# A fifth of the attention's probabilities transposed on TensorE, in a two-layer trunk on one core

## The chip, the cores and the metric

The kernel runs on one core of one Trainium2 chip. The metric is the device time of one execution in microseconds (us); less is better. Times of the kernel before are given as the median of three runs and as one profiled execution.

## The reference

The trunk has two layers on 2048 tokens of width 1024. Layer 0 mixes tokens by sliding-window attention, layer 1 by multi-head latent attention; behind each stands a mixture of experts. The change lies in layer 1's attention, for 16 heads with 64 + 32 columns of query and key and 64 of value:

```python
def block(args):
    qi, blk = args
    sc = jnp.einsum('bqhd,bkhd->bhqk', qi, k).astype(jnp.float32) * scale
    qpos = blk * Q_BLOCK + jnp.arange(Q_BLOCK)
    sc = jnp.where(kpos[None, :] <= qpos[:, None], sc, -jnp.inf)
    p = jax.nn.softmax(sc, axis=-1)
    return jnp.einsum('bhqk,bkhd->bqhd', p.astype(v.dtype), v)
```

`Q_BLOCK` is 128, so a head has 16 query blocks; block i looks at i + 1 key blocks.

## The kernel before

Float32 values are carried as two float16 tiles, a high and a low half, and a product is made of three matmuls. `attend` (L1333) does the attention of layer 1. A **unit** is one head h and one query block i. The list `units` takes, for each head, the query blocks in the order 15, 0, 14, 1, and so on; the last head takes them from 0 to 15. A unit's scores are computed in **chunks** of up to 512 keys (up to four **blocks** of 128), so two units in a row mostly have five chunks. There are 256 units, 640 chunks and 2176 blocks.

`scores` (L1381) does one chunk: three matmuls into a PSUM tile `sc` of a ring of seven (L1394 to L1396), a mask for the unit's last chunk (L1398), and the maximum of each row on DVE (L1399). Behind the last chunk DVE joins the maxima (L1404), and for each chunk ACT makes the exponential `bpr` (L1408). The probabilities must then stand with keys on the partitions, to be the stationary operand of the value matmuls. For this each chunk gets a place in a **pack** of up to 16 blocks: its high half is cast into `bpp` by DVE (L1422) or ACT (L1424), its low half is subtracted by POOL or DVE (L1425). The two shares in `SHARES` set how often DVE does the one or the other. A full pack goes out as one transposing transfer from `bpp` to `bpt`, issued on SP's queue by `turn` (L180). There are four buffers of `bpp` and five of `bpt`.

Chunks for which `direct` says so go another way. Before, these are the last three units of the last head. `turn_unit` (L1429) transposes their float32 blocks on PE against the identity (L1435) into another tile of the `sc` ring; ACT copies the high half out of PSUM (L1439) and DVE makes the low half (L1440).

`values` (L1442) multiplies a unit's transposed blocks with the values: for each block one matmul with the high half (L1454) and one with the low half (L1455), summed in the PSUM tile `po`. At a pair's end DVE reduces `po` to `ou` (L1461). `finish` normalises a pair of heads and transposes it with smaller transfers (`oT`).

The main loop goes over the units n. It calls the scores of unit n and the values of unit n - LAG, LAG being 4, chunk by chunk in turns, and behind them `turn_unit` of unit n - 1:

```python
for c in range(max(ns, nv)):
    if c < ns:
        scores(n, h, i, U[n], c)
    if c < nv:
        values(hv, iv, n - LAG, U[n - LAG], c)
if n - 1 in U and U[n - 1]["pr"]:
    turn_unit(U[n - 1])
```

The order of the instructions in each engine's queue is not just that of these calls: it is set while the program is built, by a scheduler that reckons with its own times of the engines. On the chip each queue runs in that order.

Of the kernel before, what the change touches and what calls it, by code (L numbers as in the profile page):

```python
# [12 lines left out]
F16 = mybir.dt.float16  # L13
# [8 lines left out]
P = 128  # L22
# [5 lines left out]
B_H, QR, KVR, NOPE, ROPE = 16, 384, 256, 64, 32  # L28
# [92 lines left out]
class Kernel:  # L121
# [1211 lines left out]
    def attend(self, q_d, kr_d, o_d, w_o):  # L1333
        nc, tc = self.nc, self.tc
        V, G, C = nc.vector, nc.gpsimd, nc.scalar
        LAG, PACK, SHARES = 4, 16, (1 / 3, 1 / 6)
        with ExitStack() as s:
            kp = s.enter_context(tc.tile_pool(name="tb", bufs=1, reuse_waits="tile"))
            wk = s.enter_context(tc.tile_pool(name="tk", bufs=2, reuse_waits="tile"))
# [3 lines left out]
            qb = [self.t(kp, [96, 2, S], F16, f"qb{n}") for n in range(2)]  # L1343
            for n in range(3):
                nc.sync.dma_start(kb[n][NOPE:], kr_d)
            U, heads, todo, owed = {}, {}, [], [0.0, -150.0]

            pack = {"n": 0}

            def room():  # L1350
                return self.t(ps, [P, 512], F32, "sc", bufs=7)

            def place(nb):
                if pack["n"] + nb > PACK:
                    send()
                if pack["n"] == 0:
                    pack["pp"] = self.t(wk, [P, PACK, 2, P], F16, "bpp", bufs=4)
                    pack["pt"] = self.t(wk, [P, PACK, 2, P], F16, "bpt", bufs=5)
                at = pack["n"]
                pack["n"] += nb  # L1360
                return pack["pp"][:, at:at + nb], pack["pt"][:, at:at + nb]

            def send():
                n, pp, pt = pack["n"], pack["pp"], pack["pt"]
                if n:
                    self.turn(pt[:, :n].rearrange("p k s q -> p (k s) q"), pp[:, :n].rearrange("p k s q -> p (k s q)"))
                pack["n"] = 0
# [6 lines left out]
                for u in range(2):  # L1374
                    nc.sync.dma_start(qb[e][64 + 16 * u:80 + 16 * u], q_d[g, 2][64 * u + 16 * n:64 * u + 16 * n + 16])

            def direct(h, i):

                return h == B_H - 1 and i >= 13

            def scores(n, h, i, u, c):  # L1381

                (Qh, Ql), (Kh, Kl) = ([b[h % len(b)][:, x] for x in range(2)] for b in (qb, kb))
                qs = slice(i * P, (i + 1) * P)
                nk = (i + 1) * P
                ncn = -(-nk // 512)
                if c == 0:
                    u["sm"], u["sc"], u["pt"], u["pr"] = self.t(wk, [P, 8], F32, "bsm2", bufs=4), [], [], []
                sm = u["sm"]
                w = min(512, nk - 512 * c)  # L1390
                ks = slice(512 * c, 512 * c + w)
                sc = room()
                last = c == ncn - 1
                nc.tensor.matmul(sc[:, :w], Qh[:, qs], Kh[:, ks], start=True, stop=False)  # L1394
                nc.tensor.matmul(sc[:, :w], Qh[:, qs], Kl[:, ks], start=False, stop=False)  # L1395
                nc.tensor.matmul(sc[:, :w], Ql[:, qs], Kh[:, ks], start=False, stop=not last)  # L1396
                if last:
                    nc.tensor.matmul(sc[:, w - P:w], self.ident_b, self.causal, start=False, stop=True)  # L1398
                V.tensor_reduce(sm[:, c:c + 1], sc[:, :w], axis=AX.X, op=ALU.max, negate=ncn == 1)  # L1399
                u["sc"].append((sc, w))  # L1400
                if not last:
                    return
                if ncn > 1:
                    V.tensor_reduce(sm[:, 4:5], sm[:, 0:ncn], axis=AX.X, op=ALU.max, negate=True)  # L1404
                nm = sm[:, 4:5] if ncn > 1 else sm[:, 0:1]
                for sc, w in u["sc"]:
                    pr = self.t(wk, [P, 512], F32, "bpr", bufs=7)
                    C.activation(pr[:, :w], sc[:, :w], AF.Exp, bias=nm)  # L1408
                    if direct(h, i):
                        u["pr"].append((pr, w))  # L1410
                        continue
                    pp, pt = place(w // P)
                    u["pt"].append(pt)
                    pb = pr[:, :w].rearrange("p (k q) -> p k q", q=P)

                    mine = [False, False]
                    for part, share in enumerate(SHARES):
                        owed[part] += share * w
                        if owed[part] > w / 2 and not (part and mine[0]):
                            mine[part], owed[part] = True, owed[part] - w  # L1420
                    if mine[0]:
                        V.tensor_copy(pp[:, :, 0], pb)  # L1422
                    else:
                        C.activation(pp[:, :, 0], pb, AF.Copy)  # L1424
                    (V if mine[1] else G).tensor_tensor(pp[:, :, 1], pb, pp[:, :, 0], op=ALU.subtract)  # L1425
                if n % 2 and (h == B_H - 1 or n == len(units) - 1):
                    send()

            def turn_unit(u):  # L1429

                pt = self.t(wk, [P, PACK, 2, P], F16, "bpt", bufs=5)
                for c, (pr, w) in enumerate(u["pr"]):
                    tp = room()
                    for k in range(0, w, P):
                        nc.tensor.transpose(tp[:, k:k + P], pr[:, k:k + P], self.ident)  # L1435
                    out = pt[:, 4 * c:4 * c + w // P]
                    u["pt"].append(out)
                    tp = tp[:, :w].rearrange("p (k q) -> p k q", q=P)
                    C.activation(out[:, :, 0], tp, AF.Copy)  # L1439
                    V.tensor_tensor(out[:, :, 1], tp, out[:, :, 0], op=ALU.subtract)  # L1440
# [63 lines left out]
            for n in range(len(units) + LAG):  # L1504
                ns = nv = 0
                if n < len(units):
                    h, i = units[n]
# [9 lines left out]
                    if at == 0 and h % 2 and h + 2 < B_H:  # L1517

                        out = [(kb[(h + 1 + e) % 3], slice(64 * e, 64 * e + 64)) for e in range(2)]
# [9 lines left out]
# [7 lines that stand above are left out]
# [116 lines left out]
```

## Time and profile before

| what | us |
|---|---|
| median of three runs | 3699.47 (3691.94 to 3699.72) |
| the profiled execution | 3693.81 |
| its span, first to last instruction | 3692.1 |

The span falls into stages that a table of windows shows. Busy times in us:

| stage, us from the span's start | length | PE | DVE | ACT | POOL | granted clock |
|---|---|---|---|---|---|---|
| 0 to 680: layer 0's attention | 680 | 565.37 | 497.22 | 343.64 | 281.09 | 0.93 |
| 680 to 1400: its experts | 720 | 622.03 | 567.30 | 465.45 | 215.80 | 0.95 |
| 1400 to 1720: latents of layer 1 | 320 | 235.58 | 236.74 | 133.32 | 184.60 | 0.86 |
| 1720 to 2627: attention of layer 1 | 907 | 731.77 | 716.42 | 620.68 | 616.21 | 0.91 |
| 2627 to 2760: projection | 133 | 118.69 | 95.49 | 21.69 | 43.17 | 0.97 |
| 2760 to 3560: experts | 800 | 682.99 | 618.26 | 475.97 | 244.94 | 0.94 |
| 3560 to 3692: last sum and norm | 132 | 0.00 | 96.72 | 49.63 | 103.96 | 0.51 |

A matmul's row is longer than the time by which it delays the next, since matmuls overlap. SP computes nothing; the time of its rows is that for which an issue holds its queue. "DMA bpt<-bpp" as the end of a wait means that the transposed pack had not landed.

### The profile page before, as it was taken

To read this page: it belongs to the slowest core of one execution; us is meant where nothing else is said; L and a number is where in the kernel's file an instruction comes from. 1 tells how busy PE (TensorE), PEld (TensorE's weight loads), DVE (VectorE), ACT (ScalarE), POOL (GpSimd) and SP (SyncE) were. 2 spreads that over 40 slices of the span, in tenths; PEclk is the share of its full clock that TensorE was granted. 3 is DMA by queue.
4 is the path that set the end of the run, shared out by engine and by line. 5 is a ranking of instruction groups with operands and counts; after the bars stand their busy time and mean duration, and the time that the engine had idled before them with its cause. 6 is when DMAs were issued, how large, how long until landed. Compare 5 with 4: busy or idle time off the path is not lost. (4 is left out here: it accounts for less than half of the span.)

```text
span 3692.1 us, 81916 instructions
## 1 busy us (share of the span) xinstructions
PE 2956.4 (80%) x32185; PEld 2213.2 (60%) x32185; DVE 2828.1 (77%) x5265; ACT 2110.4 (57%) x3613; POOL 1689.8 (46%) x1655
## 2 busy tenths in 40 slices
PE   7888798499998884798888888878886799988840
PEld 3454443399988882344555555554443799888840
DVE  5777768688877786785877878778586788787768
ACT  6676621266666674444766767667311566666744
POOL 3444434323323236664767767667234123222358
PEclk9999899799999997799999989999898899999975
DMA  7887689799999997997999999999897899999985
GB/s 207 171 167 154 128 249 308 242 322 346 351 360 356 350 372 238 215 227 166 190 190 204 193 196 203 188 199 208 201 304 222 293 347 351 369 360 362 361 321 205
DMA packets 1214676, 959.43 MB, mean 260 GB/s; under 512 B 1039072, under 2 KB 1097696, under 8 KB 1163360
## 3 DMA queue, kind: packets, MB, share of 16 engines
q1 hardware_dynamic: 1179456, 836.56, 85.9%
q0 software_dynamic: 34816, 117.47, 8.8%
q8 instruction: 256, 4.19, 0.4%
q14 instruction: 148, 1.21, 0.1%
HBM read 538.32 MB, written 159.65 MB: 189 GB/s over the span
## 5 line engine op out<-in xcount | busy, mean ns | idle before, releaser
L176 DVE SCALAR_TENSOR_TENSOR wl<-raw,wh 128x2048 f16<-128x2048 f32 x322 | 831.7, 2586 | 204.3 <-ACT wh L171 204.1
L900 PE MATMUL pg<-xt,wh 128*128 128x128 f16 (+5 forms) x4096 | 821.6, 231 | 57.5 <-POOLq L862 30.3
L902 PE MATMUL pg<-xt,wl 128*128 128x128 f16 (+5 forms) x4096 | 808.6, 231 | 45.7 <-DVE wl L176 45.7
L901 PE MATMUL pg<-xt,wh 128*128 128x128 f16 (+5 forms) x4096 | 821.0, 231 | 0.0
L171 ACT ACTIVATE wh<-raw 128x2048 f16<-128x2048 f32 x384 | 723.8, 1901 | 124.7 <-DMA raw<-in_moe_w_dram 108.3
L1425 POOL TENSOR_TENSOR bpp<-bpr,bpp 128x512 f16<-128x512 f32 (+3 forms) x513 | 544.7, 1083 | 244.8 <-DVE bpp L1422 160.2
L928 POOL DMA_DIRECT2D y<-yr x256 | 145.3, 569 | 710.7 <-DVE yr L920 459.1
L918 PE MATMUL py<-hh,wl 128*128 128x128 f16 (+5 forms) x2048 | 415.7, 231 | 48.5 <-POOL wl L174 48.5
L1408 ACT ACTIVATE bpr<-sc,bsm 128x512 f32<-128x512 f32 (+3 forms) x640 | 356.3, 626 | 166.2 <-DVE bsm L1404 157.0
L902 PEld LDWEIGHTS <-wl 128*128 128x128 f16 x4096 | 403.4, 99 | 56.4 <-DVE wl L176 56.3
L900 PEld LDWEIGHTS <-wh 128*128 128x128 f16 x4096 | 405.9, 99 | 42.0 <-issue 33.1
L917 PE MATMUL py<-hl,wh 128*128 128x128 f16 (+5 forms) x2048 | 415.3, 231 | 10.9 <-DVE hl L174 10.9
L1399 DVE TENSOR_REDUCE bsm<-sc 128x1 f32<-128x512 f32 (+3 forms) x640 | 369.4, 600 | 70.5 <-PE sc L1396 52.9
L901 PEld LDWEIGHTS <-wh 128*128 128x128 f16 x4096 | 406.1, 99 | 18.7 <-issue 18.7
L916 PE MATMUL py<-hh,wh 128*128 128x128 f16 (+5 forms) x2048 | 413.8, 230 | 0.7 <-ACT hh L171 0.7
L174 POOL TENSOR_TENSOR wl<-raw,wh 128x2048 f16<-128x2048 f32 x62 | 256.0, 4129 | 260.5 <-ACT wh L171 230.9
L1454 PE MATMUL po<-v,bpt 128*128 128x130 f16 x2176 | 244.8, 231 | 148.2 <-DMA bpt<-bpp 138.0
L1454 PEld LDWEIGHTS <-bpt 128*128 128x128 f16 x2176 | 209.1, 103 | 186.8 <-DMA bpt<-bpp 170.7
L1394 PE MATMUL sc<-kb,qb 96*128 96x512 f16 (+3 forms) x640 | 238.5, 373 | 29.2 <-ACT bpr L1408 15.6
L918 PEld LDWEIGHTS <-wl 128*128 128x128 f16 x2048 | 202.7, 99 | 66.7 <-POOL wl L174 54.9
L1395 PE MATMUL sc<-kb,qb 96*128 96x512 f16 (+3 forms) x640 | 237.5, 371 | 0.0
L1455 PE MATMUL po<-v,bpt 128*128 128x65 f16 x2176 | 236.7, 201 | 0.0
(324 smaller groups left out, 7685.0 us busy)
## 6 DMA issues: line engine op xcount, KB each, us to landing
raw<-in_moe_w_dram SPq DMA_DIRECT2D x384, 1024.0 KB
y<-yr POOLq DMA_DIRECT2D x256, 192.0 KB
x<-pxr SPq DMA_DIRECT2D x32, 512.0 KB
cz<-x SPq DMA_DIRECT2D x32, 512.0 KB
xs<-zero SPq DMA_DIRECT2D x32, 384.0 KB
q<-qn SPq DMA_DIRECT2D x48, 256.0 KB
ax<-in_x_t_dram SPq DMA_DIRECT2D x16, 512.0 KB
o<-aoT SPq DMA_DIRECT2D x16, 512.0 KB
```

Of the source, the lines that this page charges most:

```text
L171: nc.scalar.activation(hi, src, AF.Copy, scale=scale)
L176: eng.scalar_tensor_tensor(lo, src, scale, hi, op0=ALU.mult, op1=ALU.subtract)
L900: nc.tensor.matmul(out, hi, x[:, c], start=c == 0, stop=False)
L901: nc.tensor.matmul(out, hi, x[:, KC + c], start=False, stop=False)
L902: nc.tensor.matmul(out, lo, x[:, c], start=False, stop=c == KC - 1)
L916: nc.tensor.matmul(out, hi, hh[:, m], start=m == 0, stop=False)
L917: nc.tensor.matmul(out, hi, hl[:, m], start=False, stop=False)
L918: nc.tensor.matmul(out, lo, hh[:, m], start=False, stop=m == F // P - 1)
L1399: V.tensor_reduce(sm[:, c:c + 1], sc[:, :w], axis=AX.X, op=ALU.max, negate=ncn == 1)
L1408: C.activation(pr[:, :w], sc[:, :w], AF.Exp, bias=nm)
L1425: (V if mine[1] else G).tensor_tensor(pp[:, :, 1], pb, pp[:, :, 0], op=ALU.subtract)
L1454: nc.tensor.matmul(po, pt[:, k % 4, 0], vv, start=k == 0, stop=False)
```

## The change

`direct` now also picks chunks of all other units: a running account grows by a fifth of each chunk's width, and a chunk is turned on TensorE when the account exceeds half its width. Such a chunk is not put into a pack; it keeps its number in the unit, its transposes stand behind the scores of the next unit, and its halves go into a small tile `bpd` of a ring of three (a unit with several such chunks still takes a `bpt`). The share of high halves cast by DVE goes from 1/3 to 2/5 of the rest, that of low halves subtracted by DVE from 1/6 to 1/16.

```diff
-        LAG, PACK, SHARES = 4, 16, (1 / 3, 1 / 6)
+        LAG, PACK, SHARES, TURNED = 4, 16, (2 / 5, 1 / 16), 1 / 5
...
-            def direct(h, i):
-
-                return h == B_H - 1 and i >= 13
+            def direct(h, i, w):
+
+                owed[2] += TURNED * w
+                if h == B_H - 1 and i >= 13:
+                    return True
+                if owed[2] > w / 2:
+                    owed[2] -= w
+                    return True
+                return False
...
-                    if direct(h, i):
-                        u["pr"].append((pr, w))
+                    if direct(h, i, w):
+                        u["pr"].append((len(u["pt"]), pr, w))
+                        u["pt"].append(None)
                         continue
...
             def turn_unit(u):
-                pt = self.t(wk, [P, PACK, 2, P], F16, "bpt", bufs=5)
-                for c, (pr, w) in enumerate(u["pr"]):
+                whole = self.t(wk, [P, PACK, 2, P], F16, "bpt", bufs=5) if len(u["pr"]) > 1 else None
+                for c, pr, w in u["pr"]:
                     tp = room()
                     for k in range(0, w, P):
                         nc.tensor.transpose(tp[:, k:k + P], pr[:, k:k + P], self.ident)
-                    out = pt[:, 4 * c:4 * c + w // P]
-                    u["pt"].append(out)
+                    if whole is None:
+                        out = self.t(wk, [P, 4, 2, P], F16, "bpd", bufs=3)[:, :w // P]
+                    else:
+                        out = whole[:, 4 * c:4 * c + w // P]
+                    u["pt"][c] = out
```

By these rules 471 blocks in 156 chunks are turned on TensorE (45 in 12 before), and the packs become 122 with 1705 blocks (143 with 2131). Lines behind L1376 move down: the scores' line is L1400 in the changed kernel, the mask's L1404, the turn L1442, the value matmuls' L1464.

The order of the queues moves too. First PE's queue before, in head 4, from the last score chunk of one pack (`bpt_27374`) to its first use: the mask that ends each unit's scores, and the first value matmul of that pack.

```order
L1398 MATMUL sc_27422<-causal_87,identb_83 128x128
L1398 MATMUL sc_27466<-causal_87,identb_83 128x128
L1398 MATMUL sc_27524<-causal_87,identb_83 128x128
L1398 MATMUL sc_27568<-causal_87,identb_83 128x128
L1398 MATMUL sc_27641<-causal_87,identb_83 128x128
L1398 MATMUL sc_27682<-causal_87,identb_83 128x128
L1398 MATMUL sc_27758<-causal_87,identb_83 128x128
L1394 MATMUL sc_27784<-kb_2525_23787,qb_2527_23789 128x512
L1394 MATMUL sc_27797<-kb_2525_23787,qb_2527_23789 128x512
L1454 LDWEIGHTS bpt_27374
```

Behind the pack's last chunk PE finishes six units' scores and begins a seventh's, 17 chunks, before it takes the pack.

The same place in the changed kernel, PE's queue, one pack (`bpt_27522`) of the same head, with the transposes of turned chunks (`bpr`) and the small tile's use left out:

```order
L1404 MATMUL sc_27542<-causal_87,identb_83 128x128
L1442 MATMUL sc_27557<-ident_75,bpr_27533 128x128
L1404 MATMUL sc_27602<-causal_87,identb_83 128x128
L1404 MATMUL sc_27647<-causal_87,identb_83 128x128
L1442 MATMUL sc_27660<-ident_75,bpr_27609 128x128 x4
L1404 MATMUL sc_27708<-causal_87,identb_83 128x128
L1442 MATMUL sc_27738<-ident_75,bpr_27658 128x128
L1404 MATMUL sc_27758<-causal_87,identb_83 128x128
L1464 LDWEIGHTS bpt_27522
L1464 MATMUL po_27686<-v_2129_20955,bpt_27522 128x130
```

Now four units' scores, 10 chunks, lie between the pack's last score chunk and its first use, and three turns of chunks.

## Rows read from the trace of the kernel before

**Rows 1.** Source view of the scores' and value lines, attention: count, min/median/max ns, first and last start.

```profile
L1394 PE MATMUL sc<-kb,qb x640: 216/379/635, 1726.0 to 2611.5; 96*128 96x512 f16 x98, 96*128 96x128 f16 x31, 96*128 96x384 f16 x16, 96*128 96x256 f16 x15
...
L1454 PE MATMUL po<-v,bpt x2176: 217/220/316, 1748.6 to 2624.4; 128*128 128x130 f16 x198
```

**Rows 2.** Windows view, attention: length, busy us and instructions of each engine, clock, DMA.

```profile
1720.00:2627.00 907.00, 731.77 (x7420) 480.87 (x7421) 716.42 (x1503) 620.68 (x1207) 616.21 (x601) 0.91 1.08 195
```

**Rows 3.** Source view of `turn`'s line, attention: SP's transposing issues.

```profile
L180 SPq DMA_TRANSPOSE bpt<-bpp x143: 1457/4934/8116, 1741.7 to 2608.9; - x143
L180 SPq DMA_TRANSPOSE oT<-op x31: 1231/1261/1856, 1847.6 to 2616.1; - x31
```

**Rows 4.** Timeline of SP's queue, 2096.8 to 2109 us: start, length, operation.

```profile
2096.86 5.39 SPq L180 DMA_TRANSPOSE bpt<-bpp  x1
2102.34 1.28 SPq L180 DMA_TRANSPOSE oT<-op  x1
2103.72 5.00 SPq L180 DMA_TRANSPOSE bpt<-bpp  x1
```

**Rows 5.** Timeline, one pack: last score, exponentials, last subtractions, issue, first use.

```profile
1968.41 0.62 PE L1394 MATMUL sc<-kb,qb 96*128 96x512 f16 x1
...
1972.93 1.26 ACT L1408 ACTIVATE bpr<-sc,bsm 128x512 f32<-128x512 f32 x2
...
1975.94 2.46 POOL L1425 TENSOR_TENSOR bpp<-bpr,bpp 128x512 f16<-128x512 f32 x2
...
1982.54 4.84 SPq L180 DMA_TRANSPOSE bpt<-bpp  x1
...
1991.22 0.23 PE L1454 MATMUL po<-v,bpt 128*128 128x130 f16 x1 [1.69 <-DMA bpt<-bpp]
```

**Rows 6.** Groups of the attention: line, operation, count, busy us, mean ns, idle before.

```profile
L1425 POOL TENSOR_TENSOR bpp<-bpr,bpp 128x512 f16<-128x512 f32 (+3 forms) x513 | 544.7, 1083 | 244.8 <-DVE bpp L1422 160.2 <-ACT bpp L1424 49.5 <-DVE bsm L1404 12.7
...
L1424 ACT ACTIVATE bpp<-bpr 128x512 f16<-128x512 f32 (+2 forms) x404 | 220.8, 589 | 26.6 <-DMA bpt<-bpp 26.3
...
L1422 DVE CAST bpp<-bpr 128x512 f16<-128x512 f32 (+3 forms) x224 | 133.5, 596 | 27.5 <-ACT bpr L1408 15.0 <-DMA bpt<-bpp 9.4 <-POOL bpp L1425 2.2
L1425 DVE TENSOR_TENSOR bpp<-bpr,bpp 128x512 f16<-128x512 f32 (+3 forms) x115 | 101.1, 879 | 0.9 <-ACT bpp L1424 0.9
...
L1440 DVE TENSOR_TENSOR bpt<-sc,bpt 128x512 f16<-128x512 f32 (+2 forms) x12 | 7.4, 648 | 1.7 <-ACT bpt L1439 1.7
...
L1439 ACT ACTIVATE bpt<-sc 128x512 f16<-128x512 f32 (+2 forms) x12 | 6.4, 570 | 2.2 <-PE sc L1435 2.1
```

**Rows 7.** PE's transposes: source view, two timeline rows, and windows around these for the clock.

```profile
L1435 PE MATMUL sc<-ident,bpr x45: 272/330/457, 2591.4 to 2620.5; 128*128 128x128 f32 x45
...
2591.37 0.66 PE L1435 MATMUL sc<-ident,bpr 128*128 128x128 f32 x4
...
2612.82 2.77 PE L1435 MATMUL sc<-ident,bpr 128*128 128x128 f32 x12
...
2591.30:2592.10 0.80, 0.72 (x6) 0.42 (x4) 0.76 (x2) 0.59 (x2) 0.00 (x0) 1.00 1.26 252
2612.80:2615.60 2.80, 2.80 (x17) 2.74 (x16) 2.80 (x8) 1.19 (x2) 0.10 (x1) 0.50 0.99 218
```

**Rows 8.** Timeline, a pack that met SP almost free: score, subtraction, issue, use.

```profile
2379.56 0.22 PE L1394 MATMUL sc<-kb,qb 96*128 96x128 f16 x1
...
2387.26 1.15 POOL L1425 TENSOR_TENSOR bpp<-bpr,bpp 128x512 f16<-128x512 f32 x1
...
2389.11 4.87 SPq L180 DMA_TRANSPOSE bpt<-bpp  x1
...
2395.86 0.23 PE L1454 MATMUL po<-v,bpt 128*128 128x130 f16 x1 [0.31 <-DMA bpt<-bpp]
```

**Rows 9.** Waits of the attention: total us, times, longest.

```profile
PE po L1454 <- DMA bpt<-bpp: 138.0, 79, 5.4
DVE ou L1461 <- PE po L1455: 74.9, 50, 4.6
```

More of the change, by code (lines that the diff above doesn't have):

```diff
@@ L1345, in attend @@
                 nc.sync.dma_start(kb[n][NOPE:], kr_d)
-            U, heads, todo, owed = {}, {}, [], [0.0, -150.0]
+            U, heads, todo, owed = {}, {}, [], [0.0, -150.0, 0.0]
             pack = {"n": 0}
```

## Prediction

> **What bounds the kernel now.** The table of stages says where to look: the change touches only the attention of the second layer. By the source view of the score line its first score matmul starts at 1726.0 us, and by the group of the value line the last value matmul at 2624.4 [rows 1], a stage of 898.4 us out of a span of 3692.1. It scores 640 chunks, so it takes 1.404 us a chunk, and what follows is argued in that unit. No compute engine is full there: PE 731.8 us of 907, DVE 716.4, ACT 620.7, POOL 616.2 [rows 2].
>
> SP's queue is full. A transfer that transposes one pack holds SP for 4.93 us in the median and there are 143 of them, 31 more hold it 1.26 us [rows 3]: 705 + 39 us. In a typical stretch one issue starts within 0.2 us of the end of the one before [rows 4]. So packs are bound by SP.
>
> The reader should next see how long a pack is on its way, and how far ahead PE works meanwhile. One pack of before, followed by hand [rows 5]: its last score chunk starts on PE at 1968.41; the last low half that it needs is the second of two POOL subtractions from 1975.94 to 1978.40, 10.0 us later; SP takes the pack at 1982.54, after 4.1 us behind other packs; PE uses it at 1991.22, 8.7 us later, having idled 1.69 us for it. In all 22.8 us. In the same time PE issued the scores of 17 more chunks, as the first piece of order shows. Over all 143 packs I counted on PE, by the names of the tiles, how many score chunks stand between the last one of a pack and the first value matmul that uses it: 16.1 on average, and 16.1 x 1.404 = 22.6 us, the same time from the other side. PE is an in-order queue: this **lead** is fixed by the order of the program, the pace is not.
>
> **The change part by part.** *SP.* 143 packs become 122, and 2131 blocks 1705. At 4.93 us for a mean of 14.9 blocks (0.331 us a block), SP sheds 426 x 0.331 = 141 us. Nothing of this reaches the end by itself; it does so only if SP's queue is what the next pack waits for.
>
> *ACT.* Casts go from 404 to 283 (0.589 us), PSUM copies from 12 to 156 (0.570) [rows 6]: -71 + 82 = +11 us. *DVE.* Casts 224 to 201 (0.596), subtractions 115 to 36 (0.879), PSUM subtractions 12 to 156 (0.648): -14 - 69 + 93 = +10 us. *POOL.* 513 to 448 subtractions of 1.083: -70 us. None of the three was full, so these cost nothing by themselves; their cover is the wait for packs.
>
> *PE.* 426 more transposes. Four in a row took 0.66 us, and one takes 0.33 in the median, so each behind the first adds 0.11, at a granted clock of 1.00; twelve in a row took 2.77, 0.22 each behind the first, at 0.50 [rows 7]: +47 to +94 us. I take 0.12, because the mean granted clock of the stage is 0.91 [rows 2]: 51 us. PE would then be busy about 783 us. It stays below the stage's time.
>
> *The order.* This is the term that decides. The new transposes stand on PE behind the scores of their own unit and wait for ACT's exponentials. The order that results on PE is another: the second piece of order shows two units' scores, the values of two units before them, and a transpose between; the lead of that pack is 10 chunks. Over all 122 packs it is **9.6 chunks** instead of 16.1. Five chunks make a pair of units, so a pack now has about two pairs' time to get from its last score to its use, where it had over three.
>
> What must happen in that time does not get much shorter. From the pack above, without the 4.1 us in SP's queue: 10.0 + 8.7 = 18.7 us, the long end. For the short end I take a pack that met SP almost free [rows 8]: last score at 2379.56, last subtraction done at 2388.41, issued at 2389.11, used at 2395.86 after a wait of 0.31 us. That is 16.3 us, or 15.6 without the 0.7 before SP. The flight alone, issue to use, is 6.8 to 8.7 us in the two.
>
> A pack's way of L us and a lead of 9.6 chunks give a pace of L / 9.6: 1.63 us a chunk at 15.6, **1.70 at 16.3**, 1.95 at 18.7. I take 16.3, near the short end: engines that wait longer have shorter queues, and SP's is nearly gone. The stage becomes 640 x 1.70 = 1087 us (1040 to 1247), which is +189 us (+142 to +349). Nothing else in the program changes. The profiled execution took 3693.81 us, its span 3692.1; 3693.8 + 189 = 3883. The median of the runs shown, 3699.47, lies 5.7 us above the profiled one; with half of that the forecast is **3885 us**, and the case's own range 3840 to 4050.
>
> Where the waits go: PE's 79 waits for a landed pack (138.0 us) and those of its weight loads [rows 9] grow; ACT's wait for the maxima, DVE's for the values and SP's idle time grow behind them, because scores are queued behind the waiting value matmul. That DVE waits for value matmuls already shows, 74.9 us [rows 9].
>
> The Trainium skill speaks against this change here: "DMA: Bandwidth & Descriptors", section "Rules for kernel authors", says to issue a transfer early, compute, and wait on its semaphore late. By that rule moving the wait from 16.1 to 9.6 chunks behind the pack's scores loses; the trace agrees so far, since even with the long lead PE waited 138.0 us.
>
> **The rivals.** *Faster: the freed queue decides.* SP's 141 us come back until PE is the bound: 783 us busy, and the stage has never had PE, DVE and the rest mesh without gaps; I put the stage at 845 us, between 783 and the 898.4 of now, -53 us: 3640 us at the median. For it speaks that SP is full [rows 4] and that the followed pack waited 4.1 us for it. Against: it needs a way of 845 / 640 x 9.6 = 12.7 us, and the quick pack took 16.3. Point of decision: a way below 13.5 us (9.6 x 1.404). The Trainium skill is on this side in "VectorE: DVE Perf Modes", section "Rules for kernel authors": transpose 128x128 on TensorE if PSUM will do as the destination. The trace bears out its premise, 0.11 us a block against 0.331.
>
> *No change.* The way shrinks to 13.5 us, because a pack holds 14.0 blocks instead of 14.9 and fewer subtractions stand before it; the loss and SP's gain cancel: 3699 us.
>
> *Slower still: PE waits for exponentials too.* The 144 new turned chunks are transposed 2.8 score chunks behind their own score, on average, by the order on PE. In the followed pack the chunk scored at 1968.41 had its exponential, the second of the two in that row, done at 1974.19 [rows 5]: 5.8 us. At 1.70 us a chunk there are 4.8: 1.0 us short, 144 times, is 144 us if none of it lies under the waits for packs: 4030 us.
>
> *The change does not do what it says.* The order excludes it: 471 blocks are transposed on PE, 45 before.
>
> **How the numbers follow.** Forecast 0.65, slower still 0.14, no change 0.05, faster 0.16. The faster case keeps this much because the way of 16.3 us comes from a stage in which all queues were loaded, and I have seen no pack without that load. A change of this kernel can be told from none from about 0.2% (7 us) on. So faster 0.16, same 0.05, slower 0.79. The range goes from 3660, which cuts the better part off the faster case, to 4050, the long end of the way; it leaves out some 0.14.
>
> **What would show it.** Right: the stage longer than 1000 us; SP's transposing issues 122, with idle time between them; PE's waits for the landed pack in the stage well above 138.0 us, several us each; the pace times 9.6 near 16 us. Slower still: large waits of PE on ACT's exponentials ahead of the transposes. Wrong: the stage under 890 us, PE waiting for packs less than now; the step that fails would then be the way of a pack, which must come out below 13 us.

## The result and the profile after

The changed kernel takes 3928.82 us in the median of four runs (3920.45 to 3933.91), beside 3695.7 us (3684.36 to 3699.72, four runs) for the kernel before: 1.0634 times as long, with an interval of 1.06 to 1.0668. The forecast was 3885 us, so the sign and the size came out, 44 us short. The profiled execution took 3933.91 us, its span 3932.2.

The stage of the attention first. The source view of the changed kernel, answering to [rows 1, 3] (count, min/median/max ns, first and last start):

```profile
L1400 PE MATMUL sc<-kb,qb x640: 218/379/634, 1726.6 to 2843.9; 96*128 96x512 f16 x98, 96*128 96x128 f16 x31, 96*128 96x384 f16 x16, 96*128 96x256 f16 x15
...
L1464 PE MATMUL po<-v,bpt x1750: 217/220/315, 1744.7 to 2855.9; 128*128 128x130 f16 x195
...
L180 SPq DMA_TRANSPOSE bpt<-bpp x122: 1267/4532/8492, 1738.8 to 2837.5; - x122
```

From the first score to the last value matmul of a pack it is 2855.9 - 1726.6 = 1129.3 us, where it was 898.4 [rows 1]: 231 us more, nearly the whole of the 240 us between the spans of the two profiled executions (3932.2 and 3692.1). The pace is 1129.3 / 640 = 1.765 us a chunk. The way of a pack, again pace times lead, is 1.765 x 9.57 = 16.9 us (9.57 is the lead unrounded).

The windows view of the stage, answering to [rows 2] (length, then busy us of PE, PEld, DVE, ACT and POOL, the granted clock, the DMA share, GB/s):

```profile
1720.00:2858.00 1138.00, 837.10 (x7843) 565.18 (x7843) 707.42 (x1545) 627.45 (x1229) 538.81 (x536) 0.87 0.68 130
```

PE is busier by 105 us, POOL less by 77; ACT and DVE did not move by 10. No compute engine is full, and the DMA share, the time of the DMA packets as a share of 16 engines' time, fell from 1.08 [rows 2] to 0.68. SP, which was full before [rows 4], now stands idle between packs. Its queue in a typical stretch of the changed kernel:

```profile
2195.30 0.53 SPq L1498 DMA_DIRECT2D ob<-oT  x1
2196.41 5.46 SPq L180 DMA_TRANSPOSE bpt<-bpp  x1
2201.97 1.25 SPq L180 DMA_TRANSPOSE oT<-op  x1
2203.39 4.93 SPq L180 DMA_TRANSPOSE bpt<-bpp  x1
2208.38 0.58 SPq L1498 DMA_DIRECT2D ob<-oT  x1
2214.86 4.82 SPq L180 DMA_TRANSPOSE bpt<-bpp  x1
```

Behind 2208.96 nothing is ready for 5.9 us. Over the stage SP's stretches of more than 1 us without an issue are 107 with 465 us in sum, where they were 13 with 44 us. What SP was relieved of did not become speed, because the packs now come later than SP could take them.

The pack that SP takes at 2203.39, followed by its other rows in the timeline, as in [rows 5, 8]:

```profile
2193.61 0.38 PE L1400 MATMUL sc<-kb,qb 96*128 96x512 f16 x1
...
2197.64 2.68 ACT L1414 ACTIVATE bpr<-sc,bsm 128x512 f32<-128x512 f32 x5 [1.02 <-DVE bsm L1410]
...
2199.43 0.55 PE L1442 MATMUL sc<-ident,bpr 128*128 128x128 f32 x3 [2.93 <-ACT bpr L1414]
...
2200.88 1.13 DVE L1432 TENSOR_TENSOR bpp<-bpr,bpp 128x512 f16<-128x512 f32 x1 [0.17 <-ACT bpp L1431]
...
2207.51 0.22 PE L1464 MATMUL po<-v,bpd 128*128 128x130 f16 x1 [0.54 <-DVE ou L1471]
...
2210.10 0.23 PE L1464 MATMUL po<-v,bpt 128*128 128x130 f16 x1 [1.73 <-DMA bpt<-bpp]
```

Last score at 2193.61, the last low half done at 2202.01, issued 1.4 us later, used 6.7 us after that: 16.5 us in all. Meanwhile PE stood still three times: 2.93 us for an exponential that it was to transpose, 0.54 for DVE's reduction of `po`, 1.73 for the pack itself. While it stands, the scores behind it do not start, and the packs after this one get later too. The same three legs as means over all packs, each pack followed by the place of its instructions in the queues:

| leg, mean us | before | after | quick pack of [rows 8] |
|---|---|---|---|
| last score to last low half | 10.9 | 8.9 | 8.8 |
| wait for SP | 4.4 | 0.8 | 0.7 |
| issue to first use | 8.0 | 7.7 | 6.8 |
| sum | 23.3 | 17.4 | 16.3 |

These sums, the mean ways as measured, lie 0.5 to 0.7 us above lead times pace (16.9 and 22.6).

The waits of the stage (total us, times, longest), answering to [rows 9]:

```profile
POOL bpp L1432 <- DVE bpp L1429: 432.2, 155, 9.7
ACT bpr L1414 <- DVE bsm L1410: 268.1, 113, 7.1
...
PE po L1464 <- DMA bpt<-bpp: 148.1, 59, 6.0
DVE ou L1471 <- PE po L1465: 120.6, 66, 6.5
...
PE sc L1442 <- ACT bpr L1414: 94.8, 60, 4.8
...
PE po L1464 <- DVE ou L1471: 27.6, 25, 2.8
```

The loss, told on PE, adds up from these and one line of the kernel before:

```profile
PE po L1454 <- DVE ou L1461: 7.4, 9, 1.5
```

From the first score to the last value matmul PE's busy time grew by 106 us, its waits for exponentials ahead of a turn by 95 (there were none), those for DVE's `ou` by 20 (7.4 before), and those for landed packs by 10 (138.0 before [rows 9]): 231 us, the other small ones cancelling. POOL, ACT and DVE wait long, but behind PE: they have nothing to do until scores come.

The groups of the split, answering to [rows 6], and the turns:

```profile
L1432 POOL TENSOR_TENSOR bpp<-bpr,bpp 128x512 f16<-128x512 f32 (+3 forms) x448 | 467.7, 1063 | 497.4 <-DVE bpp L1429 432.2 <-ACT bpp L1431 21.9 <-DVE rs L1486 17.5
...
L1442 PE MATMUL sc<-ident,bpr 128*128 128x128 f32 x471 | 97.8, 328 | 94.9 <-ACT bpr L1414 94.8
...
L1429 DVE CAST bpp<-bpr 128x512 f16<-128x512 f32 (+3 forms) x201 | 95.7, 477 | 122.4 <-ACT bpr L1414 112.0 <-issue 8.5 <-POOL bpp L1432 1.4
...
L1450 DVE TENSOR_TENSOR bpd<-sc,bpd 128x512 f16<-128x512 f32 (+3 forms) x144 | 78.4, 545 | 40.5 <-ACT bpd L1449 39.4
L1449 ACT ACTIVATE bpd<-sc 128x512 f16<-128x512 f32 (+3 forms) x144 | 71.8, 499 | 112.0 <-PE sc L1442 106.6 <-PE po L1465 5.1
```

The counts are those forecast, and the mean durations lie below the forecast ones. The 97.8 us of the turns are the lengths of their rows, which overlap.

### The profile page after: what moved, and what is told of

It reads as the page before. It is cut to its first block, busy times and chain, and to the rows that moved or that the text cites. A ratio compares the mean times of both kernels' runs of the same rounds, so it can differ in the third digit from the quotient of the medians.

```text
span 3932.2 us, 82629 instructions
## 1 busy us (share of the span) xinstructions
PE 3068.5 (78%) x32611; PEld 2295.2 (58%) x32611; DVE 2813.9 (72%) x5307; ACT 2118.9 (54%) x3636; POOL 1614.0 (41%) x1590
## 5 line engine op out<-in xcount | busy, mean ns | idle before, releaser
L1432 POOL TENSOR_TENSOR bpp<-bpr,bpp 128x512 f16<-128x512 f32 (+3 forms) x448 | 467.7, 1063 | 497.4 <-DVE bpp L1429 432.2
L1414 ACT ACTIVATE bpr<-sc,bsm 128x512 f32<-128x512 f32 (+3 forms) x640 | 348.2, 627 | 272.1 <-DVE bsm L1410 268.1
L917 PE MATMUL py<-hl,wh 128*128 128x128 f16 (+5 forms) x2048 | 415.4, 231 | 12.2 <-DVE hl L174 11.9
L1464 PE MATMUL po<-v,bpt 128*128 128x130 f16 x1750 | 220.3, 237 | 183.4 <-DMA bpt<-bpp 148.1
L1464 PEld LDWEIGHTS <-bpt 128*128 128x128 f16 x1750 | 177.9, 108 | 183.0 <-DMA bpt<-bpp 173.8
L1400 PE MATMUL sc<-kb,qb 96*128 96x512 f16 (+3 forms) x640 | 243.1, 380 | 13.8 <-DVE qn L176 8.7
L1401 PE MATMUL sc<-kb,qb 96*128 96x512 f16 (+3 forms) x640 | 240.7, 376 | 0.0
L1402 PE MATMUL sc<-kb,qb 96*128 96x512 f16 (+3 forms) x640 | 237.6, 374 | 0.0
```

The lines of the kernel that those rows point to most:

```text
L917: nc.tensor.matmul(out, hi, hl[:, m], start=False, stop=False)
L1464: nc.tensor.matmul(po, pt[:, k % 4, 0], vv, start=k == 0, stop=False)
```

## The experiments

The theory to be tested: the **lead**, the number of score chunks that PE's queue holds between a pack's last score and its first use, sets the pace together with the way of a pack. The rivals: PE's waits for exponentials ahead of a turn are the loss by themselves; or the moved shares are; or the way stretches. The table gives every run. Time and stage are us; before is the kernel before on the same chip; the turn's lead is the same count from the score of a turned chunk to its transposes, "-" where none waits for an exponential or only the last units are turned; way is lead times pace.

| run | time | before | stage | lead | turn's lead | pace | way |
|---|---|---|---|---|---|---|---|
| kernel before | 3695.7 | | 898.4 | 16.1 | - | 1.404 | 22.6 |
| changed kernel | 3928.82 | 3695.7 | 1129.3 | 9.6 | 2.8 | 1.765 | 16.9 |
| e1_shares_only | 3666.67 | 3690.04 | 876.0 | 16.7 | - | 1.369 | 22.8 |
| e2_turn_one_later | 3728.46 | 3690.04 | 922.4 | 12.2 | 5.7 | 1.441 | 17.6 |
| e3_scores_ahead | 3810.41 | 3690.04 | 1006.4 | 10.7 | 2.8 | 1.573 | 16.8 |
| e4_turn_two_later | 3722.88 | 3690.04 | 915.4 | 12.4 | 7.6 | 1.430 | 17.7 |
| e5_later_lag8 | 3660.05 | 3686.73 | 866.4 | 14.3 | 5.7 | 1.354 | 19.4 |
| e6_two_later_lag8 | 3661.75 | 3686.73 | 867.7 | 14.3 | 7.6 | 1.356 | 19.4 |
| e7_three_later_lag8 | 3651.78 | 3686.73 | 851.0 | 14.8 | 10.3 | 1.330 | 19.7 |
| e8_turn_waits_for_nothing | 3730.38 | 3686.73 | 927.0 | 12.1 | - | 1.448 | 17.6 |
| e9_lead_restored | 3661.04 | 3693.48 | 856.8 | 14.9 | 10.3 | 1.339 | 20.0 |
| e10_lead_restored_tenth | 3676.94 | 3693.48 | 871.2 | 15.3 | 9.8 | 1.361 | 20.8 |
| e11_shares_only_timed | 3673.6 | 3693.48 | 877.4 | 16.7 | - | 1.371 | 22.9 |
| e12_turn_only | 3948.76 | 3687.82 | 1143.5 | 9.3 | 2.8 | 1.787 | 16.5 |

The time of e9 is the median of six executions, that of e10 and of e11 of four; the others are one execution each. Single executions of the kernel before lay between 3683.57 and 3705.0 us on one chip, so one execution says nothing about 10 us.

### e1_shares_only: one part alone

The kernel before with the changed shares, without the turned chunks.

```diff
-        LAG, PACK, SHARES = 4, 16, (1 / 3, 1 / 6)
+        LAG, PACK, SHARES = 4, 16, (2 / 5, 1 / 16)
```

> The kernel before with the moved shares alone (2/5 and 1/16), nothing turned on TensorE but the last three units. By the order the lead of a pack is 16.7 score chunks, 16.1 before. Lead theory: packs stay bound by SP, the attention stays at 898 us within 15, the time at 3696 us within 20. Rival (the shares cost or give by themselves, since POOL now makes 15/16 of the low halves): the stage moves by more than 15 us, POOL being the engine ahead of the packs.

3666.67 us beside 3690.04: the shares are not where the loss comes from, they lie on the other side. The lead theory expected no change (3696 within 20) and missed; its rival, a stage that moves by more than 15 us, holds with 876.0 instead of 898.4. The source view of this run, stage 1714.7 to 2590.7:

```profile
L1394 PE MATMUL sc<-kb,qb x640: 218/379/634, 1714.7 to 2580.6; 96*128 96x512 f16 x98, 96*128 96x128 f16 x31, 96*128 96x384 f16 x16, 96*128 96x256 f16 x15
...
L1454 PE MATMUL po<-v,bpt x2176: 217/220/315, 1735.5 to 2590.7; 128*128 128x130 f16 x198
```

### e2_turn_one_later: the turn behind the scores of one more unit

```diff
-                if n - 1 in U and U[n - 1]["pr"]:
-                    turn_unit(U[n - 1])
+                if n - 2 in U and U[n - 2]["pr"]:
+                    turn_unit(U[n - 2])
```

> The changed kernel with a unit's chunks turned one unit later, all else the same. By the order the lead of a pack is 12.2 chunks (9.6 in the change), that of a turn behind its own score 5.7 (2.8). Lead theory: a pack's way of 16.9 us (9.6 x 1.765, measured in the change) over 12.2 chunks is 1.39 us a chunk, a stage of 886 us, 3690 us in all. Rival (PE's waits for the exponentials alone are the loss): these 95 us go and the waits for packs stay at 148 us, stage 1035, 3835 us in all.

3728.46 us. This one edit takes back 200 of the 233 us, but the 3690 us of the first theory were missed by 38; its rival's 3835 lies farther off still. Waits of PE in this run, the two that matter:

```profile
PE po L1464 <- DMA bpt<-bpp: 126.4, 73, 5.6
...
PE sc L1442 <- ACT bpr L1414: 1.6, 4, 0.6
```

The waits for exponentials are gone with the turn's lead of 5.7 chunks. Those for landed packs are 73 and 126.4 us. The edit moves both leads at once, the pack's from 9.6 to 12.2, so alone it does not tell the theories apart. What it does show is that the way did not shrink with the new order: 17.6 us.

### e3_scores_ahead: the pack's lead without the turn's

The scores get a higher rank with the scheduler; the turn stays behind the next unit's scores.

```diff
-                        scores(n, h, i, U[n], c)
+                        with tc.high_priority(offset=400):
+                            scores(n, h, i, U[n], c)
```

> The changed kernel with the scheduler told to prefer scores by 400 instructions. By the order the lead of a pack is 10.7 chunks (9.6 in the change), that of a turn 2.8 as in the change. Lead theory: 16.9 / 10.7 = 1.58 us a chunk, a stage of 1011 us, 3810 us in all. Rival (waits for the exponentials): nothing changes, 3929 us within 20.

3810.41 us, where 3810 was expected. Source view and PE's waits of this run (scores begin at 1720.8):

```profile
L1464 PE MATMUL po<-v,bpt x1750: 217/220/315, 1739.4 to 2727.2; 128*128 128x130 f16 x195
```

```profile
PE po L1464 <- DMA bpt<-bpp: 111.0, 49, 5.2
PE sc L1442 <- ACT bpr L1414: 60.5, 48, 4.0
```

The turn's lead is 2.8 chunks as in the changed kernel, the pack's is 10.7 instead of 9.6, and the stage is 123 us shorter. PE's waits for exponentials fell by 34 us only, those for landed packs by 37, those for `ou` by 10, its busy time by 30; small waits make up the rest. A theory in which only the turn's lead matters gives none of the 123 us, since the turn's lead is the same. (The raised rank can move other instructions too; only the two leads were counted.) The way is 16.8 us, within 0.1 of the changed kernel's.

### e4_turn_two_later: the turn's lead without the pack's

```diff
-                if n - 1 in U and U[n - 1]["pr"]:
-                    turn_unit(U[n - 1])
+                if n - 3 in U and U[n - 3]["pr"]:
+                    turn_unit(U[n - 3])
```

> The changed kernel with a unit's chunks turned two units later. By the order the lead of a pack is 12.4 chunks, as with one unit later (12.2), that of a turn 7.6 (5.7). Lead theory: as with one unit later within 15 us. Rival (waits for the exponentials): faster than with one unit later by what is left there of PE's waits for them.

3722.88 us: beside e2 the turn's lead grows from 5.7 to 7.6 chunks, the pack's hardly (12.4), and the time hardly changes. Once a turned chunk's exponential is there in time, more room for it brings nothing that one execution of each shows.

### e5, e6 and e7: eight units between scores and values

All three have LAG 8; they turn unit n - 2, n - 3 and n - 4. With values eight units behind, a later pair's values are written into a shared buffer before the last units of an earlier pair have read it, so in these three runs part of the value products is taken from another pair's values. Count and shape of the instructions are the same.

```diff
-        LAG, PACK, SHARES, TURNED = 4, 16, (2 / 5, 1 / 16), 1 / 5
+        LAG, PACK, SHARES, TURNED = 8, 16, (2 / 5, 1 / 16), 1 / 5
...
-                if n - 1 in U and U[n - 1]["pr"]:
-                    turn_unit(U[n - 1])
+                if n - 2 in U and U[n - 2]["pr"]:
+                    turn_unit(U[n - 2])
```

> Chunks turned one unit later and LAG 8 in place of 4. By the order the lead of a pack is 14.3 chunks, that of a turn 5.7 as with one unit later alone. Lead theory: the way of 17.6 us measured there over 14.3 is 1.23 us a chunk, 788 us; PE (757 us busy there) and the others don't mesh that well, so a stage of about 850 us, 3655 us in all, below the kernel before. Rival (what is left beyond 898 us is the cost of the turning itself on PE, ACT and DVE): no gain over one unit later, 3728 us within 15.

> Chunks turned two units later and LAG 8. Lead of a pack 14.3 chunks, of a turn 7.6. Lead theory: as one unit later with LAG 8 within 15 us. Rival (the turn's own wait): faster than that by 10 us or more.

> Chunks turned three units later and LAG 8. Lead of a pack 14.8 chunks, of a turn 10.3. Lead theory: as the two others with LAG 8 or some 10 us better. Rival (a turn so late makes the halves of turned chunks late, and they hold PSUM and exponentials longer): worse than two units later by 15 us or more.

3660.05, 3661.75 and 3651.78 us. With leads of 14.3, 14.3 and 14.8 all three lie below the kernel before, though its lead was longer (16.1). A pack stands before SP for 1.9 to 2.1 us in the mean here and not for 4.4, which fits that the turned kernel needs less lead; but the shares alone give some 20 us (e11), so this is not shown. A way of 17.6 us held over 14.3 chunks would be 788 us of stage (640 x 17.6 / 14.3), and it was 866. So the rule ends between 12.4 and 14.3 chunks: from there on the lead alone does not set the pace. Most of the additional way (19.4 to 19.7 us) is time that a pack spends lying ready: where the trace gives the landing (37 to 77 packs of a run's 122, 41 in e2), it comes 6.9 to 7.1 us after the issue, 6.9 in e2, and the pack then lies for 1.7 to 2.0 us, 0.6 in e2. The wait for SP is longer by 0.5 to 0.7 us. LAG 8 with the turn left behind unit n - 1, and LAG 8 with nothing turned, were not run.

### e8_turn_waits_for_nothing: the dependence taken away

The turned transposes read the identity instead of the exponentials, so that they wait for none.

```diff
-                        nc.tensor.transpose(tp[:, k:k + P], pr[:, k:k + P], self.ident)
+                        nc.tensor.transpose(tp[:, k:k + P], self.ident, self.ident)
```

> The changed kernel, but PE transposes the identity in place of the exponentials, so that the transposes wait for nothing that ACT makes (the values then lack a fifth of the probabilities). The same instructions otherwise, in their order of the change's code (unit n - 1, LAG 4). By the order the lead of a pack is 12.1 chunks. Lead theory: the dependence of the turn on the exponentials costs by shortening the lead, so this runs as one unit later does (lead 12.2): 3728 us within 20. Rival (waits for the exponentials by themselves): the 95 us of these waits go and no more, 3835 us.

3730.38 us, where 3728 was expected. The same instructions on every engine, no wait of PE for an exponential ahead of a turn, and still 44 us longer than the kernel before. PE's largest waits in this run, in sum, are again for landed packs:

```profile
PE po L1464 <- DMA bpt<-bpp: 112.8, 67, 3.9
```

The scheduler, too, sees no dependence here, and its order has a lead of 12.1 chunks; e2, whose turns do depend on exponentials, has 12.2 and 3728.46 us. Two kernels with the same lead and different dependences take the same time: where the exponentials are there in time, the dependence as such costs nothing that these executions show. Of the 231 us of the change some 200 come with the dependence where the turn is due right behind the next unit's scores: there the lead falls from 12 to 9.6, and PE waits 95 us for exponentials. In e2 and e8 the short lead and these waits are gone together (1.6 us of such waits are left in e2), so this pair does not tell what each costs; only e3 moves the pack's lead with the turn's lead held. No run has a lead of 9.6 without these waits, and none the kernel before with a shorter lead and nothing turned. The other 30 to 40 us remain with the lead of 12 that turned chunks have in these orders with LAG 4. Why the scheduler sets 12 and not 16 even then is open; that it reckons with fewer packs on SP was argued, not tried.

### e9_lead_restored: a version for use

LAG 8, the turn three units later, and the work on the next values moved behind, so that it writes their buffer only when it has been read.

```diff
-        LAG, PACK, SHARES, TURNED = 4, 16, (2 / 5, 1 / 16), 1 / 5
+        LAG, PACK, SHARES, TURNED = 8, 16, (2 / 5, 1 / 16), 1 / 5
...
                         deliver(h + 1)
+                    if at == 6 and h % 2 == 0:
                         if h + 2 < B_H:
...
-                if n - 1 in U and U[n - 1]["pr"]:
-                    turn_unit(U[n - 1])
+                if n - 4 in U and U[n - 4]["pr"]:
+                    turn_unit(U[n - 4])
```

> Chunks turned three units later, LAG 8, and the weights of the next pair's values four units later, so that they come behind the last values of the pair that used the same buffer. Lead of a pack 14.9 chunks, of a turn 10.3. Lead theory: as the run with LAG 8 and turns three units later, a stage of 851 us, 3652 us within 10, faster than before by 1 %. Rival (that run gained from values read too early): slower than it by 15 us or more, not told from before.

3661.04 us (3645.35 to 3674.02) beside 3693.48 (3683.57 to 3705.0): a ratio of 0.9908, interval 0.9885 to 0.9931. Expected was 3652 within 10. It beats both kernels, the one before by 0.9%, the change by some 270 us with the same turned fifth and the same shares. Its windows view and waits:

```profile
1720.00:2580.00 860.00, 740.60 (x7843) 508.72 (x7842) 700.96 (x1545) 622.60 (x1227) 549.48 (x536) 0.95 0.93 170
```

```profile
PE po L1464 <- DMA bpt<-bpp: 59.7, 35, 4.7
...
PE po L1464 <- DVE ou L1471: 6.7, 9, 1.5
...
PE sc L1442 <- ACT bpr L1414: 1.8, 3, 0.8
```

PE runs the same 7843 instructions as in the changed kernel in 740.6 us instead of 837.1, at a granted clock of 0.95 instead of 0.87. Counted only where no earlier row of PE still runs, the turns take 82.8 us in the changed kernel, 56.6 in e9 and 7.5 before. So some 49 of the 106 us by which PE's busy time grew in the change stay in e9 as the turns' own price, and the rest is gone where PE waits less and the clock stands higher. (Before had 0.91; e9's other work on PE is 40 us shorter than before, which hides the turns' price.)

### e10_lead_restored_tenth: a tenth instead of a fifth

As e9, with half as much turned.

```diff
-        LAG, PACK, SHARES, TURNED = 8, 16, (2 / 5, 1 / 16), 1 / 5
+        LAG, PACK, SHARES, TURNED = 8, 16, (2 / 5, 1 / 16), 1 / 10
```

> As the run before it, with a tenth of the probabilities turned in place of a fifth. Lead 15.3 chunks; 128 packs in place of 122. Lead theory: with a lead of 15 the way of a pack no longer bounds it; SP is held some 90 us less than before instead of 140, and stays below the stage: within 10 us of the fifth. Rival (SP's queue bounds again): slower by 20 us or more.

3676.94 us, ratio 0.9952 (0.9935 to 0.9969): no better than the fifth, and its interval just does not meet e9's. It is 16 us slower, between the two forecasts (within 10; by 20 or more). SP's issues take 730 us of 871 here and 665 of 857 in e9, which fits that with enough lead relief of SP does turn into time; against it stands that a tenth gives no more than the shares alone (e11).

### e11_shares_only_timed: the shares again, in four executions

The kernel of e1.

```diff
-        LAG, PACK, SHARES = 4, 16, (1 / 3, 1 / 6)
+        LAG, PACK, SHARES = 4, 16, (2 / 5, 1 / 16)
```

> The kernel before with the moved shares alone, once more with rounds: the single look gave 3667 us beside 3690. Lead theory has SP as the bound of both; a way that is some us shorter would not help a full queue, so 3690 within 10. Rival (the shares give by themselves): 3667 within 10.

3673.6 us, ratio 0.9946 (0.9927 to 0.9965). Expected was 3690 within 10; the rival, that the shares give time by themselves, holds: 20 us. So of e9's 32 us some 20 are the shares', and the 12 us that are left for the turned fifth and the longer LAG together are barely told from nothing, as the two intervals overlap between 0.9927 and 0.9931. Why the shares give 20 us stays open. SP was still full, its issues taking 810 us of 877 (821 of 898 before); its transposing issues of packs were shorter in sum, 709 us beside 719, and its idle time 68 us beside 78. That accounts for the 20 us as a sum, but not for what made the issues shorter.

### e12_turn_only: the turned fifth without the shares

```diff
-        LAG, PACK, SHARES, TURNED = 4, 16, (2 / 5, 1 / 16), 1 / 5
+        LAG, PACK, SHARES, TURNED = 4, 16, (1 / 3, 1 / 6), 1 / 5
```

> The change with the shares left as they were (1/3 and 1/6), a fifth turned on TensorE as in the change. By the order the lead of a pack is 9.3 chunks, that of a turn 2.8. Lead theory: a way of 16.9 us over 9.3 is 1.82 us a chunk, a stage of 1163 us, 3960 us in all. Rival (the shares' gain of 20 us and the turning add up): 3929 + 20 = 3949, which this run does not tell apart from the lead; a second rival (the shares are what makes the change slow): near 3690.

3948.76 us; the lead of 9.3 gave 3960 before the run, simple addition of the 20 us gives 3949, so the two are not told apart. What is refuted is that the loss needs the shares. Source view and waits (scores begin at 1722.6):

```profile
L1464 PE MATMUL po<-v,bpt x1750: 217/221/315, 1739.8 to 2866.1; 128*128 128x130 f16 x195
```

```profile
PE po L1464 <- DMA bpt<-bpp: 165.3, 71, 5.9
PE sc L1442 <- ACT bpr L1414: 96.1, 54, 5.2
```

It looks like the changed kernel in these rows, with more waits for landed packs at a shorter lead.

## Why the prediction was right, and where it was off

**The bound of before.** SP's full queue was read rightly: its issues took 821 of 898 us, and with less on it SP has 465 us of idle stretches. So was the conclusion that this reaches the end only if SP's queue is what the next pack waits for. The mean wait for SP fell from 4.4 to 0.8 us, and the time grew all the same. What made SP's issues long the prediction did not ask: the DMA share was 1.08 in the same stage [rows 2], so it is not excluded that the transfers held up the issues; fewer packs relieve both.

**The lead.** The deciding term held. Across the change and five experiments with leads from 9.3 to 12.4 the way, lead times pace, stayed between 16.5 and 17.7 us, rising a little with the lead, while the stage went from 915 to 1143. e3 is the one that moves the pack's lead with the turn's lead held, and it came out at 3810.41 us for 3810 expected. How much of the loss PE's waits for exponentials would make at an unchanged lead was not run. The Trainium skill's rule to wait late for a transfer ("DMA: Bandwidth & Descriptors", section "Rules for kernel authors") agrees with these runs as far as they go: the later the wait, in chunks, the shorter the stage, up to some 14 chunks.

**The term that was mis-sized** is the way: 16.3 us forecast, 16.9 measured, which at a lead of 9.57 is 40 us of the 44 by which the forecast was short. The table of the legs says which part. The quick pack's first leg (8.8 us to the mean of 8.9) and its wait for SP (0.7 to 0.8) were right; the flight to the first use was 0.9 us too short, 6.8 for a mean of 7.7. The pack chosen was one for which PE waited 0.31 us, so its flight was all but bare; a mean pack probably also lies ready for some time, behind whatever PE waits for first (the changed kernel's trace does not give the landings; in e3 78 packs landed 7.0 us after the issue and lay for 1.2). That the size came out this well is in part luck. Counted over all packs of before, the quick pack's way was the shortest of 143, whose mean is 23.3 us; and the mean pack of the changed kernel, 17.4 us, put into the forecast's own formula would have given a stage of 1164 us, 34 too long, because lead times pace lies 0.5 us below the mean way.

**Two steps failed in the list of what would show it.** PE's waits for landed packs were to grow well above 138.0 us; they are 148.1 in 59 waits. They became fewer and longer (2.5 us each, 1.7 before), and PE meets another wait beside them: the exponentials, 94.8 us in 60. The rival "slower still" had that mechanism and priced it at 144 waits of 1.0 us on top of all others; it came as 60 of 1.6 us, and not on top: the stage was only 42 us longer than the forecast's 1087. That PE's wait for an exponential lets the next pack land meanwhile is argued, not shown; in e3, with the same turn's lead and 1.1 chunks more for the pack, both waits shrank.

And PE was to be busy for 783 us; it was 837. Counted only where no earlier row of PE still runs, the turns grew by 75 us (7.5 to 82.8) where the sum had 51, and all other work of PE by 31 where it had nothing. A transpose took 0.12 us in the sum; in the changed kernel it took 0.15 in the mean where the granted clock was 1.00 and 0.24 where it was 0.50. In e9 it took 0.12 at 1.00, so the clock is not all of it; that a transpose behind a wait has no earlier row to overlap with is the likely rest, not shown. The 31 us go with the clock, which the sum took from before: it stood at the lower level for 289 us of the stage, 164 before, and a value matmul's row added 0.09 us at the lower level and 0.05 at the higher. In e9, with the same instructions and a clock of 0.95, PE was busy for 741 us.

**The shifts priced at nothing** were about as large as forecast: POOL shed 77 us (70 forecast), ACT gained 7 (11), DVE lost 9 (10 more were forecast, but its casts took 477 ns in the mean instead of 596). SP shed 167 us (141 forecast; 719 us of transposing issues became 552). That they cost nothing by themselves is shown for the moved shares (e1, e11), not for the rest.

**The rivals.** The freed queue did not decide at a lead of 9.6. Its condition, a way shorter than the lead times the old pace, can't be tested with a way that is counted as lead times pace: that e9's 20.0 us lie below 14.9 x 1.404 = 20.9 says only that e9 is faster. The way measured leg by leg, 20.4 us in e9 and 17.4 in the changed kernel, lies on the right side in both (below 20.9, above 13.5). What spoke for the Trainium skill's advice to transpose 128x128 on TensorE ("VectorE: DVE Perf Modes", section "Rules for kernel authors"), the lower time of a block, holds too: in the changed kernel the turns cost PE 82.8 us for 471 blocks, 0.18 us each, and the issues SP 552 us for 1705, 0.32 each. The advice gains here, if at all, only in an order with a long lead: 3661.04 us with such an order, of which gain the shares alone give 20, and 3928.82 in the order of the change.

**Left open:** what sets the pace above 14 chunks, where no compute engine is full (PE 741 us of 860), the way stretches and the DMA share is 0.93; whether the turned fifth gains anything beside LAG 8; why the order has 12 chunks and not 16 even without the dependence; where the shares' 20 us come from. And since pace times lead is the way by definition, what the runs show is that the way stayed within 0.6 us of 17.1 as the lead changed, not a law for other leads.

## What to carry to other kernels

Before work is moved off a full queue, count in the order of the in-order engine how much work stands between the last step that feeds a transfer and its first use, before and after; divide the time that a transfer's whole way takes by that count, and compare with the pace of now. A new dependent step on that engine is paid for not only by its own time but by the order that it makes the scheduler choose, so put it far enough behind its producer (here one unit later was enough: 5.7 chunks and not 2.8) and count again. Price the way by several packs that are typical of the load to come, not by one whose every leg was short.

## What the runs showed of the hardware that was not expected

DVE's rows were longer where POOL worked. Casts of one shape, 128x512, took 478 ns in the mean in the changed kernel, 576 in e9 and 625 before; POOL was busy for 539 of 1138 us, 549 of 860 and 616 of 907 in the same windows. Taken one by one, such casts with no row of POOL beside them took 417 to 424 ns in the mean in each of these kernels, in e2 and in e11; those with POOL at work for their whole length took 644 to 805 (only four of them in the changed kernel), single ones from 408 to 1394. In the changed kernel 104 of 142 met no work of POOL, before 68 of 135. So the mean moved with how many of them met POOL; by what means POOL slows them is not shown. TensorE's granted clock, in these views a mean of its two levels of 1.2 and 2.4 GHz (0.50 and 1.00), went with the waits: 0.87 in the changed kernel's stage, where PE was busy in 837 of 1138 us, and 0.95 in e9's, where the same instructions kept it busy in 741 of 860.
